# A decoder layer on one core: the mixers' output operands are read early and in pieces, and SyncE's issues keep the program's order inside the slots

## The chip, the core and the metric

The kernel runs on one core of a Trainium2 chip. Its engines are TensorE (PE in the profile, with its weight loads as PEld), VectorE (DVE), ScalarE (ACT), GpSimd (POOL) and SyncE (SP), which here issues the DMAs. The metric is the device time of one execution in microseconds.

## The reference, cut

One layer of a decoder, 1024 tokens of width 1024, everything in float32. Two groups of heads mix the tokens side by side, four mLSTM heads of width 128 and eight forgetting-attention heads of width 64. Their outputs are joined, multiplied by `w_out` and added to `x`. Cross-attention into 256 memory tokens and a squared-ReLU MLP follow.

```python
mh = mlstm_chunkwise(mq, mk, mv, ig, lf)          # 4 heads
ml_out = (mh.reshape(B, S, ML_W) * jax.nn.sigmoid(ml_o))
fx_out = forgetting_attention(fq, fk, fv, flf)    # 8 heads, causal, decayed
x = x + jnp.concatenate([ml_out, fx_out], axis=-1) @ w_out[l]
x = x + cross_attention(rmsnorm(x, ln_x[l]), rmsnorm(mem, ln_mem[l]), w_xq[l], w_xkv[l], w_xo[l])
u = jax.nn.relu(rmsnorm(x, ln2[l]) @ w_ff1[l])
x = x + (u * u) @ w_ff2[l]
return rmsnorm(x, ln_f)
```

## The kernel before

Activations lie with features on the 128 partitions and tokens along the row, in two halves of 512 tokens (`hf`). A float32 product is made of three matmuls of split operands (`mm3`, L192 to L194): each operand is cut into a high part, made by ScalarE (L138, or L971 in the slots), and a low part, the difference, made by VectorE or GpSimd (L139, L972).

The stage of interest is the forgetting stage, built of slots. Each call of `slot` does one value step of attention (transposes L793, the product with the values L813) and one score step some 13 slots ahead (L754, L755; maximum L761; exponential L767; scaling L778). Beside these it runs a share of other work from a generator (`filler`), so that TensorE has something to do: eight key units and four value units of cross-attention, and then 16 output units (`out_unit`), which multiply `w_out`'s first five row blocks with the mixers' output. Output units 0 to 7 belong to the first half of the tokens, 8 to 15 to the second. A unit takes its weights from `wr`, two buffers of raw weights: `cut_half` (L971, L972) splits one in two halves, and after the second half `raw_load` (L959) reads the next into the buffer just freed.

The mixers' outputs go through a DRAM tensor `mix[hf, part, :, k]`, where k is the block of 128 features: k 0 to 3 from the mLSTM heads, stored before the stage, and one further k for each two forgetting heads, stored in it (`fx_store`, L828 and L829, from buffers `r_y` and `r_f`). The output units read k 0 to 4 back. Before the change this happens when the first unit of each half runs (and for the second half at unit 4): `mix_load` (L875) reads four blocks into a buffer of the `act` pool, 1024 KB for each part, and `mix_tile` (L881) reads the fifth into a `z` buffer.

The queries and keys of the forgetting heads also come back from DRAM (`fqk`, `decay`), eight reads for a head, into two stacks of operands that heads use in turn. `score_parts` puts the reads of head hd+2 into a list `coming` when head hd has been scored, and each slot issues one of them (`fx_step`, L728). The list also carries the eight reads of `x`'s first half into `kept`, to which the output units of the first half add their sums. The units of the second half read their piece of `x` (L932) into small buffers `r_p`, `r_b`, `r_a` and store the sums in `x1d` (L942). After the slots, `mix_load` reads the remaining three blocks (768 KB a part), and `out_rest` finishes the product.

What sets the order: the code is traced, and a scheduler places each engine's instructions by its own reckoning. Inside the slots `in_order` ties each instruction of TensorE, ScalarE, VectorE and GpSimd to the one traced before it on the same engine. SyncE was not among them, so its issues stood where the scheduler put them. SyncE works off its queue in order: an issue that waits holds all behind it.

Of the kernel before, what the change touches and what calls it, by code (L numbers as in the profile page):

```python
# [9 lines left out]
F32 = mybir.dt.float32  # L10
F32R = mybir.dt.float32r
# [5 lines left out]
COMPUTE = (mybir.EngineType.PE, mybir.EngineType.Activation, mybir.EngineType.DVE, mybir.EngineType.Pool)  # L17
P = 128
T = 1024
TH = 512  # L20
D = 1024
KT = D // P
NM = 256
MLH = 4
FXH = 8
# [3 lines left out]
KX = 1  # L29
# [15 lines left out]
def hybrid_layer(ctx: ExitStack, tc: tile.TileContext, a: dict, out: bass.AP):  # L45
# [13 lines left out]
    def sb(tag, shape, bufs, dt=F32):  # L59
        return pool.tile(shape, dt, tag=tag, name=name(tag), bufs=bufs)  # L60

    def act(dt=F32R):
        return sb("act", [P, 8, TH], 7, dt)
# [8 lines left out]
    def w4(shape=(P, 1024), dt=F32):  # L72
        t = sb("w4", [P, 1024], 5, dt)[: shape[0]]
        return t.rearrange("p (a b) -> p a b", b=shape[2]) if len(shape) == 3 else t

    def z4():
        return sb("z4", [P, T + 3], 2)
# [24 lines left out]
    def mm():  # L102

        tag = banks[turn[0] % len(banks)]
        turn[0] += 1
        return ps_tile(tag)
# [4 lines left out]
    load = nc.sync.dma_start  # L111
# [33 lines left out]
    last_of = {}  # L145

    @contextmanager
    def in_order():

        traced = nc.cur_bb.bb.instructions  # L150
        last = traced[-1]
        yield
        start = next(k for k in reversed(range(len(traced))) if traced[k] is last) + 1
        for i in traced[start:]:
            if i.engine not in COMPUTE:
                continue
            if i.engine in last_of:
                tc.add_manual_dep(
                    i,
                    last_of[i.engine],  # L160
                    mybir.DependencyInfo(mybir.DependencyClass.NoSync, mybir.DependencyReason.DATA),
                    reason="in_order",
                )
            last_of[i.engine] = i.name


    def rotate(*tags):

        spare[tags] = spare.get(tags, -1) + 1
        return w2(tags[spare[tags] % len(tags)])  # L170
# [25 lines left out]
    def both(pair, f):  # L196
        return f(pair[0]), f(pair[1])
# [137 lines left out]
    for k in range(KT):  # L335
        if k % 2 == 0:
            c = slice(k % 4 * 256, k % 4 * 256 + 512)
# [44 lines left out]
    z, e, q, lf = (small[:, i:j].rearrange("p (t c) -> p t c", c=c) for i, j, c in ((0, 128, GC), (128, 224, GW), (224, 320, GW), (320, 416, GW)))  # L382
# [192 lines left out]
    mix = dram.tile([2, 2, P, KT, TH], F32, name="mix")  # L575
# [129 lines left out]
    for _ in range(2):  # L705
        t = act().rearrange("p a b -> p (a b)").rearrange("p (i c) -> p i c", i=4)
# [5 lines left out]
    coming = []  # L712

    def fx_load(hd):

        n, e = divmod(hd, 2)
        hs = stacks[hd % 2]
        rng = slice(e * FXD, e * FXD + FXD)
        lo_, up = slice(0, FXD), slice(FXD, P)
        for rows_, i, which, part in ((lo_, 0, 0, 0), (up, 0, 0, 1), (lo_, 1, 1, 0), (up, 1, 1, 0), (up, 2, 0, 0), (up, 3, 1, 1)):  # L720
            coming.append((hs[rows_, i], fqk[which, part, n, rng, :]))
        for at_, i, sign in ((0, 2, 0), (32, 3, 1)):
            coming.append((hs[at_ : at_ + 2, i], decay[sign, :, MLH + hd, :]))
# [105 lines left out]
        load(mix[hf, 1, :, MLH + hd // 2], lo.bitcast(F32))  # L829

    rooms = {}

    def score_parts():

        for hd in range(FXH):
            for hf in range(2):
                if hf:
                    t = act(F32).rearrange("p a b -> p (a b)").rearrange("p (i c) -> p i c", i=4)
                    rooms[hd, hf] = [t[:, d, : (5 + d) * P] for d in range(4)]
                else:  # L840
                    t = [w4((P, 2, TH)) for _ in range(2)]
                    rooms[hd, hf] = [t[d // 2][:, d % 2, : (1 + d) * P] for d in range(4)]
                for d in range(4):
                    x = Tile(hd, 4 * hf + d, rooms[hd, hf][d])
                    for e in range(len(x.parts)):
                        yield x, e
            if hd + 2 < FXH:
                fx_load(hd + 2)
            if 0 < hd < 5:
                coming.extend((kept[:, n], a["x"][:, n, :TH]) for n in (2 * hd - 2, 2 * hd - 1))  # L850

    def fv_load(hd):
        t = w4((P, 8, P), F32R)
# [18 lines left out]
    def mix_load(k0, k1, hf):  # L872
        t = act().rearrange("p (e k) c -> p e k c", e=2)
        for p_ in range(2):
            load(t[:, p_, : k1 - k0].bitcast(F32), mix[hf, p_, :, k0:k1])  # L875
        return [(t[:, 0, k], t[:, 1, k]) for k in range(k1 - k0)]

    def mix_tile(k, hf):
        t = z4()[:, :T].bitcast(F32R).rearrange("p (e c) -> p e c", e=2)
        for p_ in range(2):  # L880
            load(t[:, p_].bitcast(F32), mix[hf, p_, :, k])  # L881
        return t[:, 0], t[:, 1]

    late = []

# [34 lines left out]

        return [a["w_xv"][hd, i] for i in range(2)], run

    mixes = {}

    def out_unit(hf, n):
        def run(ws):
            if n == 0 and hf == 0 or n == 4 and hf == 0:
                mixes[n // 4] = mix_load(0, MLH, n // 4) + [mix_tile(k, n // 4) for k in range(MLH, MLH + KX)]
            x = kept[:, n]
            if hf:  # L930
                x = rotate("p", "b", "a", "p", "b")
                load(x, a["x"][:, n, TH:])  # L932
            w = both(ws[0], lambda t: t.rearrange("p (k c) -> p k c", k=MLH + KX))
            ps = mm()
            for k in range(MLH + KX):
                mm3(ps, both(w, lambda t: t[:, k]), mixes[hf][k], k == 0, k == MLH + KX - 1)
                yield 3.0, k == MLH + KX - 1, lambda: sink(x, ps)

        def sink(x, ps):
            v.tensor_tensor(out=x, in0=ps, in1=x, op=ALU.add)  # L940
            if hf:
                load(x1d[:, n], x)  # L942

        return [a["w_out_a"][n]], run
# [51 lines left out]
    stores, topped = [], []  # L996

    def slot(values, until):
        with in_order():
            todo_ = late[:]  # L1000
            late.clear()
            closing = bool(ended)
            sums = []
            while ended:
                sums.append(fx_close(*ended[0]))
                hd, hf, _ = ended.pop(0)
                if hd % 2:
                    stores.append((hd, hf, True))
            x = next(steps_, None) if values else None
            if x:  # L1010
                x.turn()
            mask()

            while adds and not closing and len(adds) >= (LAG if x else 1):
                y = adds.pop(0)
                y.add()
                if y.last:
                    ended.append((y.hd, y.hf, y.ov))
                    break
            tops = scored[:]  # L1020
            scored.clear()
            for t, e in tops:
                t.top(e)
            if x:
                x.cut()
                adds.append(x)
            for f in sums:
                f()
            exps = topped[:]
            topped[:] = tops  # L1030
            for t, e in exps:
                t.exp(e)
            while exped:
                exped.pop(0).scale()
            exped.extend(t for t, e in exps if e == len(t.parts) - 1)
            fx_step()
            part = next(parts, None)
            if part:
                part[0].score(part[1])
                scored.append(part)  # L1040
            late.extend(filter(None, [f() for f in todo_]))
            if stores and stores[0][2]:
                stores[0] = (*stores[0][:2], False)
            elif stores:
                fx_store(*stores.pop(0)[:2])
            while spent[0] < until:
                step = next(fill, None)
                if step is None:
                    break
                spent[0] += step[0]  # L1050
                if step[1]:
                    late.append(step[2])
                    break
            n, e = divmod(halves[0], 2)
            if until and n < len(sources) and (e or sum(u >= now[0] for u, _ in sources[:n]) < 3):
                cut_half()
        return x
# [9 lines left out]
    token_major(a["w_fv"], fv_sink, between={4: lambda: next(closing, None)})  # L1067
    hm = act().rearrange("p a b -> p (a b)").rearrange("p (e k c) -> p e k c", e=2, k=KT)
    kept = act(F32)
    load(hm.bitcast(F32), hmd)  # L1070
    banks[:] = ["mm", "m2"]
    raw_load()
# [2 lines left out]
    n = 0  # L1075
# [7 lines left out]
    for step in fill:  # L1083
        n, e = divmod(halves[0], 2)
# [246 lines left out]
    for n in range(KT):  # L1331
# [7 lines left out]
        k = n % 4  # L1339
# [150 lines left out]
    for at, (p_, i) in enumerate(jobs):  # L1490
# [19 lines left out]
        b, k = todo[p_][:2]  # L1510
# [53 lines left out]
    for at, (b, m) in enumerate(steps):  # L1564
# [14 lines left out]
        x = x2[m // 2][:, m % 2]  # L1579
# [16 lines left out]
    for i in range(2):  # L1596
        t = act()
# [132 lines left out]
```

## Time and profile before

| what | value |
|---|---|
| three runs, median (lowest, highest) | 1522.5 us (1521.36, 1523.13) |
| profiled execution | 1519.66 us |
| its span, first to last instruction | 1517.6 us |
| TensorE busy | 1501.4 us, 99% of the span |
| VectorE, ScalarE, GpSimd busy | 1103.2, 716.6, 438.5 us |
| DMA | 288.32 MB, 190 GB/s on average |
| granted TensorE clock | 0.998 |

A page of the profile gives such sums over the whole execution. The views used below are the lists of waits (who waited for whom, in total, how often, the longest), the timelines (start, duration, engine, line, output and inputs; in brackets the idle time of the engine before it and what ended it) and windows (busy times of the engines in a stretch). A row of SyncE in a timeline is the issue of a DMA, not its transfer. Busy TensorE is an upper figure, since matmuls overlap and their ends are modelled.

### The profile page before, as it was taken

How to read it: one execution, taken by the hardware profiler on the slowest of the kernel's cores; microseconds unless marked ns; L12 is line 12 of the kernel's file. 1: busy time of each engine (PE TensorE's matmuls, PEld its weight loads, DVE VectorE, ACT ScalarE, POOL GpSimd, SP SyncE). 2: the span in 40 equal slices, each digit the busy share in tenths (PEclk: the TensorE clock that was granted, in tenths of full speed). 3: DMA queues.
4: the chain of work that ended last, by engine and by line, in shares of the span. 5: the costliest groups of instructions: out<-in, count | busy, mean ns of one | idle time of the engine just before them, and what ended most of it. 6: DMA issues, size and time to landing. Idle time of an engine off the chain costs nothing.

```text
span 1517.6 us, 21814 instructions
## 1 busy us (share of the span) xinstructions
PE 1501.4 (99%) x7708; PEld 1259.1 (83%) x7708; DVE 1103.2 (73%) x1741; ACT 716.6 (47%) x1345; POOL 438.5 (29%) x497
## 2 busy tenths in 40 slices
PE   9999999999999999999999999999999999999997
PEld 8888888889898888888888887788888888888887
DVE  7676676665798875844457888788887788777765
ACT  7343343334678763543443456565556432222124
POOL 0003030413455541011110033343333544333312
PEclk9999999999999999999999999999999999999999
DMA  6332323436897928634333436776775966555623
GB/s 212 112 115 89 118 100 124 133 125 179 253 296 225 310 89 285 228 108 130 124 110 126 163 122 237 276 276 238 273 254 215 364 260 222 222 222 214 256 85 111
DMA packets 113489, 288.32 MB, mean 190 GB/s; under 512 B 12626, under 2 KB 27276, under 8 KB 107236
## 3 DMA queue, kind: packets, MB, share of 16 engines
q1 hardware_dynamic: 113092, 286.82, 55.4%
q8 instruction: 60, 0.98, 0.3%
q14 instruction: 49, 0.40, 0.1%
q10 hardware_dynamic: 288, 0.11, 0.0%
HBM read 194.36 MB, written 92.53 MB: 189 GB/s over the span
## 4 chain that ended last, share of the span: by engine, by line
PE 61%; DVE 2%; DMA 2%; issue 1%; ACT 1%; POOL 1%; SPq 0%; POOLq 0%; DVEq 0%; ACTq 0%
PE sc L192 5%; PE sc L194 5%; PE sc L193 5%; PE tp L192 5%; PE tp L194 5%; PE tp L193 5%; PE m L193 4%; PE m L192 4%; PE m L194 4%; PE mm L193 4%; PE mm L192 4%; PE mm L194 4%; PE ov L192 2%; PE ov L194 2%; PE ov L193 2%
## 5 line engine op out<-in xcount | busy, mean ns | idle before, releaser
L193 PE MATMUL tp<-act,wh 128*128 128x512 f32 (+1 forms) x456 | 178.7, 392 | 0.0
L192 PE MATMUL tp<-act,wl 128*128 128x512 f32 (+1 forms) x456 | 178.6, 392 | 0.0
L194 PE MATMUL tp<-act,wh 128*128 128x512 f32 (+1 forms) x456 | 178.5, 392 | 0.0
L138 ACT ACTIVATE wh<-wr 128x1024 fp32r<-128x1024 f32 (+3 forms) x96 | 92.7, 967 | 98.4 <-PE tp L194 36.5
L139 DVE TENSOR_TENSOR wl<-wr,wh 128x1024 fp32r<-128x1024 f32 (+3 forms) x96 | 114.3, 1192 | 15.3 <-ACT wh L138 15.2
L192 PE MATMUL mm<-act,wl 128*128 128x512 f32 (+1 forms) x320 | 122.8, 384 | 0.0
L193 PE MATMUL mm<-act,wh 128*128 128x512 f32 (+1 forms) x320 | 122.5, 383 | 0.0
L194 PE MATMUL mm<-act,wh 128*128 128x512 f32 (+1 forms) x320 | 122.2, 382 | 0.0
L192 PE MATMUL m<-act,wl 128*128 128x512 f32 (+1 forms) x312 | 119.6, 383 | 0.3 <-DVE wl L139 0.3
L193 PE MATMUL m<-act,wh 128*128 128x512 f32 (+1 forms) x312 | 119.0, 381 | 0.7 <-DMA act<-mix 0.7
L194 PE MATMUL m<-act,wh 128*128 128x512 f32 (+1 forms) x312 | 119.0, 381 | 0.0
L192 PE MATMUL sc<-act,wl 128*128 128x512 f32 (+1 forms) x268 | 103.9, 388 | 0.0
L193 PE MATMUL sc<-act,wh 128*128 128x512 f32 (+1 forms) x268 | 103.7, 387 | 0.0
L194 PE MATMUL sc<-act,wh 128*128 128x512 f32 (+1 forms) x268 | 103.7, 387 | 0.0
L194 PEld LDWEIGHTS tp<-act,wh 128*128 128x128 f32 x456 | 85.7, 188 | 19.5
L192 PEld LDWEIGHTS tp<-act,wl 128*128 128x128 f32 x456 | 85.7, 188 | 19.1 <-DVE w L1374 0.3
L193 PEld LDWEIGHTS tp<-act,wh 128*128 128x128 f32 x456 | 85.8, 188 | 18.8
L1464 POOL TENSOR_TENSOR z<-wr 128x256 f32<-128x256 f32 x56 | 54.1, 986 | 147.1 <-DMA wr<-w_ff2q 135.2
L138 ACT ACTIVATE w<-wr 128x768 fp32r<-128x768 f32 (+2 forms) x31 | 25.5, 824 | 132.1 <-PE tp L194 69.1
L138 ACT ACTIVATE wh<-z 128x1024 fp32r<-128x1024 f32 (+2 forms) x55 | 52.5, 956 | 65.7 <-POOL z L1464 30.5
L139 DVE TENSOR_TENSOR wl<-z,wh 128x1024 fp32r<-128x1024 f32 (+2 forms) x55 | 65.9, 1199 | 11.3 <-ACT wh L138 11.2
L194 PEld LDWEIGHTS mm<-act,wh 128*128 128x128 f32 x320 | 60.1, 188 | 12.5
(673 smaller groups left out, 4197.3 us busy)
## 6 DMA issues: line engine op xcount, KB each, us to landing
act<-right SPq DMA_DIRECT2D x35, 1024.0 KB
right<-r_d SPq DMA_DIRECT2D x70, 256.0 KB
right<-w SPq DMA_DIRECT2D x56, 256.0 KB
wr<-w_ff2q SPq DMA_DIRECT2D x28, 512.0 KB
act<-fqk SPq DMA_DIRECT2D x48, 256.0 KB
wr<-w_in SPq DMA_DIRECT2D x20, 512.0 KB
wr<-w_ff SPq DMA_DIRECT2D x20, 512.0 KB
fqk<-r_p SPq DMA_DIRECT2D x32, 256.0 KB
```

The source lines that it names most:

```text
L138: s.activation(hi, src, AF.Copy)
L139: return v.tensor_tensor(out=lo, in0=src, in1=hi.bitcast(F32), op=ALU.subtract)
L192: nc.tensor.matmul(ps, w[1], x[0], start=first, stop=False, skip_group_check=more)
L193: nc.tensor.matmul(ps, w[0], x[1], start=False, stop=False, skip_group_check=more)
L194: nc.tensor.matmul(ps, w[0], x[0], start=False, stop=last, skip_group_check=more)
L1464: g.tensor_tensor(out=o, in0=x, in1=y, op=op)
```

## The change

Three things. `in_order` takes the engines as an argument, and a slot passes SyncE too, as long as it has a value step or is one of the 13 slots before the first value step; the slots after the last value step don't. `mix_load` and `mix_tile` for the output units give way to `mix_ahead`, which claims the buffers of a half and returns ten reads of one block and one part each, 256 KB. The list `extra` says after which head's score step they join `coming`: the first half's ten after heads 2, 3 and 4, the second half's ten after head 6. The eight reads of `x`'s first half are spread anew, after heads 1, 4 and 5.

```diff
-    def in_order():
+    def in_order(engines=COMPUTE):
...
-            if i.engine not in COMPUTE:
+            if i.engine not in engines:
                 continue
...
-            if 0 < hd < 5:
-                coming.extend((kept[:, n], a["x"][:, n, :TH]) for n in (2 * hd - 2, 2 * hd - 1))
+            if hd == FXH - 2:
+                extra[hd].extend(mix_ahead(1))
+            coming.extend(extra[hd])
...
-    def mix_tile(k, hf):
-        t = z4()[:, :T].bitcast(F32R).rearrange("p (e c) -> p e c", e=2)
-        for p_ in range(2):
-            load(t[:, p_].bitcast(F32), mix[hf, p_, :, k])
-        return t[:, 0], t[:, 1]
+    mixes = {}
+
+    def mix_ahead(hf):
+        t = act().rearrange("p (e k) c -> p e k c", e=2)
+        z = [z4()[:, :T].bitcast(F32R).rearrange("p (e c) -> p e c", e=2) for _ in range(KX)]
+        mixes[hf] = [(t[:, 0, k], t[:, 1, k]) for k in range(MLH)] + [(y[:, 0], y[:, 1]) for y in z]
+        return [(mixes[hf][k][p_], mix[hf, p_, :, k]) for k in range(MLH + KX) for p_ in range(2)]
...
     def out_unit(hf, n):
         def run(ws):
-            if n == 0 and hf == 0 or n == 4 and hf == 0:
-                mixes[n // 4] = mix_load(0, MLH, n // 4) + [mix_tile(k, n // 4) for k in range(MLH, MLH + KX)]
...
     def slot(values, until):
-        with in_order():
+        with in_order(COMPUTE + (mybir.EngineType.SP,) * (values or not until)):
...
     kept = act(F32)
+    residual = [(kept[:, n], a["x"][:, n, :TH]) for n in range(KT)]
+    operands = mix_ahead(0)
+    for hd, more in ((1, residual[:4]), (2, operands[:4]), (3, operands[4:8]), (4, operands[8:] + residual[4:6]), (5, residual[6:])):
+        extra[hd].extend(more)
```

TensorE's and GpSimd's instructions stand in the same order as before; on VectorE and ScalarE a few neighbours change places at the end of the stage. What moves is SyncE's queue. In the middle of the stage it read before (`wr` is a unit's weights, `fvd` the values of a head, `kxd` and `vxd` stores of the key and value units):

```order
L854 DMA w4_798_4731<-fvd_512 128x1024
L828 DMA mix_509<-r_y_794_4715 128x512
L919 DMA vxd_96<-r_p_793_4711 256x1x256
L829 DMA mix_509<-r_f_690_4252 128x512
L881 DMA z4_1134_6201<-mix_509 128x512
L959 DMA wr_804_4761<-w_xv 128x1024
L881 DMA z4_1134_6201<-mix_509 128x512
L959 DMA wr_818_4823<-w_xk 128x1024
```

Now the same weights (`wr_806`) stand there like this:

```order
L923 DMA vxd_96<-r_p_795_4715 256x1x256
L828 DMA mix_509<-r_y_796_4719 128x512
L829 DMA mix_509<-r_f_692_4254 128x512
L856 DMA w4_800_4735<-fvd_512 128x1024
L728 DMA act_500_3176<-fqk_511 64x1024
L959 DMA wr_806_4765<-w_xv 128x1024
L728 DMA act_500_3176<-fqk_511 64x1024
L728 DMA act_500_3176<-decay_508 2x1024
L959 DMA wr_820_4827<-w_xk 128x1024
L728 DMA act_500_3176<-decay_508 2x1024
L728 DMA act_589_3833<-mix_509 128x512
```

The two reads of `mix` into `z` (L881), which fetch the block that the two stores above them (L828, L829) write, are gone from the weights' neighbourhood; a read of values and a read of the next head's queries stand ahead of the weights instead.

At the end of the stage, where the first output units of the second half add `x`, SyncE's queue before (`x1d` is the store of a unit's sum):

```order
L959 DMA wr_1229_6607<-w_out_a 128x640
L875 DMA act_1269_6846<-mix_509 128x1536 x2
L942 DMA x1d_3184<-r_p_1221_6574 128x512
L959 DMA wr_1244_6680<-w_out_a 128x640
L828 DMA mix_509<-r_y_1246_6688 128x512
L932 DMA r_p_1261_6780<-x 128x512
L829 DMA mix_509<-r_f_1200_6492 128x512
L942 DMA x1d_3184<-r_b_1240_6658 128x512
```

and now:

```order
L959 DMA wr_1229_6619<-w_out_a 128x640
L877 DMA act_1269_6858<-mix_509 128x1536 x2
L942 DMA x1d_3184<-r_p_1221_6586 128x512
L932 DMA r_b_1240_6670<-x 128x512
L959 DMA wr_1244_6692<-w_out_a 128x640
L932 DMA r_b_1257_6766<-x 128x512
L828 DMA mix_509<-r_y_1246_6700 128x512
L932 DMA r_p_1261_6792<-x 128x512
L829 DMA mix_509<-r_f_1200_6504 128x512
```

The reads of `x` into `r_b` for units 1 and 4 of the second half, which stood near the stage's beginning before, now stand here, the first behind the store of unit 0's sum.

More of the change, by code (lines that the diff above doesn't have):

```diff
@@ L831, in hybrid_layer @@
     rooms = {}
+    extra = [[] for _ in range(FXH)]
     def score_parts():
@@ L921, in value_unit @@
         return [a["w_xv"][hd, i] for i in range(2)], run
-    mixes = {}
     def out_unit(hf, n):
         def run(ws):
-            if n == 0 and hf == 0 or n == 4 and hf == 0:
-                mixes[n // 4] = mix_load(0, MLH, n // 4) + [mix_tile(k, n // 4) for k in range(MLH, MLH + KX)]
             x = kept[:, n]
```

## The prediction

> **What bounds the kernel now.** I read the page first, then the list of waits of TensorE and of its weight loads, then the timelines around each wait that the change can touch, and back from those to SyncE.
>
> From the page: the span and the busy times of the whole program.
>
> ```profile
> span 1517.6 us, 21814 instructions
> PE 1501.4 (99%) x7708; PEld 1259.1 (83%) x7708; DVE 1103.2 (73%) x1741; ACT 716.6 (47%) x1345; POOL 438.5 (29%) x497
> ```
>
> TensorE is the bound: 1517.6 - 1501.4 = 16.2 us of the span are not matmul. A change that leaves its instructions and their order alone, as this one does, can win only idle time of TensorE in the forgetting stage (391 to 578 us) and what follows it. The next view is the waits of the weight loads between 391 and 606 us (who, for whom: us in total, times, the longest). I take these because matmuls overlap and a short hold shows there more fully.
>
> ```profile
> PEld sc L754 <- ACT act L767: 3.5, 3, 2.2
> PEld tp L793 <- DVE r_e L139: 2.2, 3, 1.1
> PEld m L193 <- DMA act<-mix: 1.1, 1, 1.1
> PEld tp L793 <- DVE w L139: 0.6, 2, 0.5
> PEld sc L754 <- ACT w L767: 0.6, 1, 0.6
> ```
>
> Together 8.0 us: that is all that there is to win, half a percent. Two single waits are the largest, 2.2 and 1.1 us. TensorE's timeline shows both (start, duration; in brackets the idle time before and who ended it):
>
> ```profile
> 456.51 0.40 PE L813 MATMUL ov<-r_d,w 128*128 128x512 f32 x1
> 458.68 0.50 PE L754 MATMUL sc<-act 128*128 128x512 f32 x1 [1.77 <-ACT act L767]
> ...
> 507.56 0.40 PE L192 MATMUL m<-act,wl 128*128 128x512 f32 x1
> 508.63 0.50 PE L193 MATMUL m<-act,wh 128*128 128x512 f32 x1 [0.67 <-DMA act<-mix]
> ...
> 584.06 0.39 PE L194 MATMUL m<-z,wh 128*128 128x512 f32 x1
> 584.29 0.40 PE L192 MATMUL mm<-act,wl 128*128 128x512 f32 x1
> ```
>
> Each matmul is 512 columns wide. The last two rows show undisturbed ones of that width: they start 0.23 us apart. So the first hold cost 458.68 - 456.51 - 0.23 = 1.94 us and the second 508.63 - 507.56 - 0.23 = 0.84 us.
>
> **The cause of the first hold.** ScalarE's exponentials were late because it stood waiting for a weight tile; its timeline:
>
> ```profile
> 453.05 0.26 ACT L767 ACTIVATION_READ_ACCUMULATOR act<-sc,c_mx 128x1 f32 x1
> 457.06 0.63 ACT L971 ACTIVATE wh<-wr 128x512 fp32r<-128x512 f32 x1 [3.75 <-DMA wr<-w_xv]
> ```
>
> That tile's buffer was free when VectorE ended the subtraction that last read it; the read was issued only at 453.07, after a read of the mixers' output. VectorE's row, then SyncE's timeline, then the row of SyncE's own waits:
>
> ```profile
> 448.49 0.86 DVE L972 TENSOR_TENSOR wl<-wr,wh 128x512 fp32r<-128x512 f32 x1 [0.37 <-ACT wh L971]
> 449.88 0.32 SPq L829 DMA_DIRECT2D mix<-r_f  x1
> 452.65 0.32 SPq L881 DMA_DIRECT2D z<-mix  x1
> 453.07 0.37 SPq L959 DMA_DIRECT2D wr<-w_xv  x1
> ...
> SPq L881 <- DMA mix<-r_y: 2.4, 1, 2.4
> ```
>
> The buffer was free at 448.49 + 0.86 = 449.35. SyncE came to the read of mix (L881) at 450.2, waited 2.4 us until the store of the same bytes had landed, and the weights behind it left 3.72 us late. ScalarE waited 3.75 us, TensorE 1.94 us: there were about 1.8 us of slack between them.
>
> **The change, part by part.** (a) Order within the slots. In the new order the read of mix into z is gone from this place; ahead of the weights now stand the two stores, a 512 KB read of values and one 256 KB read of queries. None of these needs a store of this moment, and all belong to work earlier in the slot than the subtraction that frees the weights' buffer. So the weights leave at about 449.4 instead of 453.07. Even if the values ahead of them cost 1 us in the queue, the read lands 2.6 us earlier, more than the hold. I take the whole 1.94 us; the bounds are 0 (the queue eats it, a rival below) and the 2.2 us of the weight load's row.
>
> (b) The mixers' operands for the first half are read in ten pieces of 256 KB, eight of them before that half's first unit. They were read in one go when the first output unit began:
>
> ```profile
> 498.93 1.34 SPq L875 DMA_DIRECT2D act<-mix  x2
> ```
>
> TensorE wanted them at 507.79 (507.56 + 0.23) and waited until 508.63. The two last pieces (z) go out in the slots in which the unit starts and are wanted by its fifth step, three slots later. The stage's transposes, first and last, give the length of its slots (min/median/max of one in ns, then the first and the last start):
>
> ```profile
> L793 PE MATMUL tp<-ident,act x208: 270/272/329, 395.9 to 576.4; 128*128 128x128 f32 x104
> L793 PE MATMUL tp<-ident,w x80: 270/273/329, 391.3 to 563.5; 128*128 128x128 f32 x80
> ```
>
> From 391.3 to 576.4 run 95 slots, 1.95 us each. Three are some 5.8 us, and 256 KB have taken 5.4 at the worst (below). So the 0.84 us goes whole. Bounds: 0 and the 1.1 us of its weight load's row.
>
> (c) What is late next. Four reads of x for the second half were free to go far ahead before; now the one for unit n=1 (r_b, L932) stands behind the store of unit 0's sum (x1d from r_p), which stands behind two reads of 768 KB (mix, L875). SyncE's timeline, its wait, and VectorE's add of that unit:
>
> ```profile
> 574.79 1.78 SPq L875 DMA_DIRECT2D act<-mix  x2
> 577.92 0.32 SPq L942 DMA_DIRECT2D x1d<-r_p  x1
> 583.31 0.33 SPq L932 DMA_DIRECT2D r_p<-x  x1
> ...
> SPq L932 <- DMA x1d<-r_p: 2.1, 1, 2.1
> ...
> 581.53 0.68 DVE L940 TENSOR_TENSOR r_b<-mm,r_b 128x512 f32<-128x512 f32 x1
> ```
>
> The queue at that time, first as a window (length, busy times by engine, clock, DMA share, GB/s), then by the slowest read in it, a weight tile's issue and the instruction that waited for it:
>
> ```profile
> 578.00:606.00 28.00, 28.00 (x123) 22.56 (x122) 12.26 (x17) 6.56 (x13) 3.86 (x5) 1.00 0.95 330
> ...
> 588.52 0.38 SPq L959 DMA_DIRECT2D wr<-w_out_a  x1
> ...
> 595.72 0.83 ACT L971 ACTIVATE wh<-wr 128x320 fp32r<-128x320 f32 x2 [5.66 <-DMA wr<-w_out_a]
> ```
>
> The store issued at 577.92 landed at 583.3: 5.4 us, behind 1.5 MB. A 256 KB read issued right behind it lands 0.8 us later (at the window's 330 GB/s), at 584.1. The add (0.68 us) then ends at 584.8, not 582.2, and TensorE, which starts unit 3 in that same bank at 584.29 (the row above), waits 0.5 us, with the semaphore 0.6. So +0.6 us; bounds 0 (lands by 583.6) and 2.0 (lands as late after its issue at 578.4 as that slowest read, 595.72 - 588.52 = 7.2 us: 585.6, add ends 586.3).
>
> (d) The 36 reads of queries and keys, before in bursts, now go one per slot; so do the eight reads of x for the first half. All land ahead of their use by the working in the first rival: 0. The extra issues (12 more reads, the same bytes) at about 0.4 us each are SyncE's time, which has nothing else queued: 0. The weight subtraction moved ahead of r_b's add on VectorE, and one split of the next stage moved behind a squaring; no wait of TensorE lies there: 0.
>
> Sum: -1.94 - 0.84 + 0.6 = -2.18 us. Against the profiled execution (1519.66 us, span 1517.6) that gives 1517.5; that run lay 2.84 us under the median of the three, 1522.5, so I put the difference on the median: **1520.3 us**.
>
> [...] Two more windows:
>
> ```profile
> 422.00:432.00 10.00, 9.93 (x76) 9.19 (x75) 9.27 (x21) 9.26 (x25) 5.13 (x6) 1.00 0.99 338
> 440.00:513.00 73.00, 69.91 (x509) 64.76 (x508) 63.34 (x157) 57.12 (x161) 39.00 (x60) 1.00 0.86 260
> ```
>
> From 422 to 432 us eight reads of 256 KB and a few of 512 KB moved 338 GB/s, as much as the 768 KB reads after 578 us (330): small pieces cost the queue nothing visible. [...]
>
> **The rivals.** First, slower: the stack rows of queries, keys and decay come too late. They were loaded in a burst; now the last of eight comes four slots before the head's first score, and SyncE reaches it only after a store of the same slot.
>
> ```profile
> 430.01 0.56 SPq L900 DMA_DIRECT2D kxd<-r_a  x1
> ...
> 436.45 0.28 PE L754 MATMUL sc<-act 128*128 128x256 f32 x1
> ```
>
> For head 3 the last row would leave at 430.6 (behind that store) and is wanted at 436.45: 5.85 us. It decides where landing takes longer. The 5.4 us above fit; the 7.2 us don't: 1.35 us late, for heads 3 to 7 five times, 6.8 us, so -2.2 + 6.8 = +4.6: 1527 us. For it: SyncE now stands still for every store. Against: bursts, which made landings slow, are gone. 17%.
>
> Second, no change: the weights land as late as before, since 512 KB of values and 256 KB of queries were put ahead of them; 1.94 us stay and only -0.84 + 0.6 = -0.24 remains: 1522.3 us. For it: the queue is 0.86 busy there. Against: 3.7 us of head start. 20%.
>
> Third, more: without bursts the other weights land earlier too and half of the remaining 8.0 - 2.2 - 1.1 = 4.7 us of waits goes: -2.18 - 2.35 = -4.5: 1518.0 us. Against: those waits end with VectorE, busy 63.34 of 73 us there. 18%.
>
> **How the numbers follow.** My forecast has 45%, 1519 to 1521.5. A difference under 0.2%, 3 us, is about what these timings can't tell from no change; its edges are 1519.5 and 1525.5. Faster: a third of my case, 15, and nearly all of the third rival, 17: 32%. Slower: the first rival but for a mild form, 15, and a little of the unforeseen: 16%. The rest, 52%, is within. The range reaches to the third rival with 1 us to spare and most of the way to the first: 1517.0 to 1526.0.
>
> **What would show it.** Right: no wait of score matmuls for L767 of over 1 us near 456 us; no wait for mix near 508; the weights' read within 0.5 us of the end of the subtraction that frees it; and a new wait of at most 1 us before unit 3's matmuls near 582 us, ended by L940. Wrong: waits of L754 for the stack reads at a head's first score (first rival), ScalarE still waiting over 3 us for w_xv (second), or a wait in a place that I named at nothing.

## The result: 1518.7 us, and the profile after

The changed kernel took 1518.68 us (median of 14 executions, 1516.9 to 1522.8), the kernel before 1522.1 us (14, 1519.59 to 1524.99) on the same chip: a ratio of 0.9982, with a 95% interval of 0.9974 to 0.999. On another chip the same kernel gave 0.9989 (0.9979 to 0.9998). By these ratios the change gains 2.7 and 1.7 us, at the edge of what these timings can tell from nothing. The median lies in the range that was forecast, 1.6 us under the forecast itself.

The profiled execution of the changed kernel tells another story. It took 1521.24 us, 1.6 us more than the profiled execution of before. From its page:

```profile
span 1519.5 us, 21816 instructions
...
PE 1502.5 (99%) x7708; PEld 1260.7 (83%) x7708; DVE 1103.0 (73%) x1741; ACT 716.8 (47%) x1345; POOL 441.5 (29%) x497
```

The waits of its weight loads between 391 and 606 us, the same view as in the prediction:

```profile
PEld sc L754 <- ACT act L767: 3.8, 2, 2.8
PEld tp L793 <- DVE r_e L139: 2.2, 3, 1.1
PEld mm L192 <- issue: 0.7, 1, 0.7
PEld tp L793 <- DVE w L139: 0.6, 2, 0.5
PEld sc L754 <- ACT w L767: 0.6, 1, 0.6
```

The wait for mix is gone, the wait for the bank mm has grown (0.2 us before, a row that the prediction's list leaves out), and the largest, which step (a) took away, is longer than before (2.8 against 2.2 us). SyncE's timeline shows why, and ScalarE's:

```profile
446.08 0.55 SPq L923 DMA_DIRECT2D vxd<-r_p  x1
446.74 0.55 SPq L828 DMA_DIRECT2D mix<-r_y  x1
447.38 1.02 SPq L829 DMA_DIRECT2D mix<-r_f  x1
448.49 0.40 SPq L856 DMA_DIRECT2D w<-fvd  x1
448.95 0.45 SPq L728 DMA_DIRECT2D act<-fqk  x1
449.50 0.53 SPq L959 DMA_DIRECT2D wr<-w_xv  x1
```

```profile
457.41 0.63 ACT L971 ACTIVATE wh<-wr 128x512 fp32r<-128x512 f32 x1 [4.31 <-DMA wr<-w_xv]
```

The weights' read left at 449.50, where I had put it (449.4), 3.57 us earlier than before. It was used at 457.41, later than before (457.06). It took 7.9 us, where before it took 4.0. Five transfers, 1.5 MB with the stores, were issued in the 3.4 us ahead of it. The queue's windows (length, busy times by engine, clock, DMA share, GB/s), first of the changed kernel, then of before:

```profile
448.00:452.00 4.00, 4.00 (x30) 3.74 (x30) 3.65 (x8) 4.00 (x12) 2.03 (x3) 1.00 0.96 281
452.00:456.00 4.00, 4.00 (x34) 3.82 (x32) 3.84 (x9) 1.10 (x3) 0.98 (x2) 1.00 0.99 257
```

```profile
448.00:452.00 4.00, 4.00 (x30) 3.75 (x30) 3.57 (x10) 4.00 (x12) 2.03 (x4) 1.00 1.05 382
452.00:456.00 4.00, 4.00 (x32) 3.77 (x31) 3.84 (x9) 1.31 (x4) 0.98 (x2) 1.00 0.72 232
```

With the read itself that is 2.1 MB, and at the 281 and 257 GB/s of the two windows they would take about 7.8 us, but that sum is not the account, since only 0.1 of the stores' 0.8 MB had still to move when the read was issued. The trace shows what was still ahead: each of these transfers lands in sixteen parts, and each part has its own record. The middle one of the sixteen stands at 450.27 us for the last store (`r_f`), at 452.50 for the values, at 454.03 for the queries and at 455.58 for the weights; the weights' last part landed at 457.39. So of the 7.9 us, 0.8 went to the stores, 2.2 to the values, 1.5 to the queries, 1.6 to the weights themselves and 1.8 to those of their parts that came late. Before, the last part of the values had landed at 452.00, ahead of the weights' issue; the weights' middle part stood at 456.72 and the last one at 457.04.

Why the full queue moved fewer bytes than before (257 GB/s at a share of 0.99 against 382 at 1.05) is not shown; it was not the stores, since from 452 to 456 us the queue moved reads alone. The transfers landed in the order in which they were issued (the last parts of the last store, the values, the queries and the weights at 450.77, 454.05, 455.10 and 457.39 us): the earlier issue bought a place behind the values and the queries.

TensorE's timeline then shows what came on top:

```profile
456.29 0.39 PE L813 MATMUL ov<-r_d,w 128*128 128x512 f32 x1
459.03 0.50 PE L754 MATMUL sc<-act 128*128 128x512 f32 x1 [2.36 <-ACT act L767]
...
461.79 0.63 PE L754 MATMUL sc<-act 128*128 128x512 f32 x1
462.21 0.63 PE L755 MATMUL sc<-act 128*128 128x512 f32 x1
```

After an idle time of 2.36 us, matmuls of 512 columns start 0.42 us apart, not 0.23. The windows by clock, of the changed kernel and of before:

```profile
456.00:460.00 4.00, 1.64 (x10) 1.12 (x9) 1.38 (x3) 2.59 (x8) 1.91 (x3) 1.00 0.67 201
460.00:465.00 5.00, 5.00 (x27) 4.60 (x26) 3.95 (x10) 3.31 (x10) 2.60 (x5) 0.66 0.74 229
```

```profile
460.00:465.00 5.00, 5.00 (x39) 4.52 (x38) 4.86 (x16) 4.52 (x14) 2.91 (x6) 1.00 0.84 242
```

A mean clock of 0.66 over 5 us is 3.4 us at half clock ((1 - 0.66) x 5 / 0.5), and the trace's clock record has 0.50 from 460.04 to 463.45 us. In the profiled execution of before the idle time was 1.77 us and the clock stayed at 1.00.

So two profiles cannot settle where the gain came from. The other two waits answer to the prediction. The operands of mix (b), no idle time at the first unit's start:

```profile
509.30 0.40 PE L192 MATMUL m<-act,wl 128*128 128x512 f32 x1
509.53 0.39 PE L193 MATMUL m<-act,wh 128*128 128x512 f32 x1
```

And the second half's first units (c), TensorE, then VectorE:

```profile
584.73 0.40 PE L194 MATMUL m<-z,wh 128*128 128x512 f32 x1
585.40 0.47 PE L192 MATMUL mm<-act,wl 128*128 128x512 f32 x1 [0.28 <-DVE r_b L940]
```

```profile
584.57 0.69 DVE L940 TENSOR_TENSOR r_b<-mm,r_b 128x512 f32<-128x512 f32 x1 [1.07 <-DMA r_b<-x]
```

The matmul of unit 3 started 0.67 us after the one before it instead of 0.23: 0.44 us lost, where 0.5 was forecast.

### The profile page after: what moved, and what is told of

Read it like the earlier page. It is cut to its first block, busy times and chain, and to the rows that moved or that the text cites. A ratio compares the mean times of both kernels' runs of the same rounds, so it can differ in the third digit from the quotient of the medians.

```text
span 1519.5 us, 21816 instructions
## 1 busy us (share of the span) xinstructions
PE 1502.5 (99%) x7708; PEld 1260.7 (83%) x7708; DVE 1103.0 (73%) x1741; ACT 716.8 (47%) x1345; POOL 441.5 (29%) x497
## 4 chain that ended last, share of the span: by engine, by line
PE 61%; DVE 3%; DMA 2%; issue 1%; ACT 1%; POOL 1%; SPq 0%; POOLq 0%; DVEq 0%; ACTq 0%
PE sc L192 5%; PE sc L194 5%; PE sc L193 5%; PE tp L192 5%; PE tp L194 5%; PE tp L193 5%; PE m L192 4%; PE m L194 4%; PE m L193 4%; PE mm L192 4%; PE mm L193 4%; PE mm L194 4%; PE ov L192 2%; PE ov L194 2%; PE ov L193 2%; PE ov L813 1%
```

## The experiments

Three theories stood after the result. *Issue* is step (a) as written: the earlier issue takes the hold away, and the profiled execution is an exception. *Queue* is the prediction's second rival: the weights land as late as before in every execution. *Clock* says that the hold lies near a length from which the clock halves, and that the kernels differ in how often that happens. "Slot 33" is the slot whose value tile starts near 456 us; it is the one in which ScalarE waits for w_xv. Every execution also has its mean granted clock on record.

**Both kernels again.** No edit.

> The kernel before, unchanged, for a second profile. Three theories are told apart by this call. Issue: what is gained is the hold of TensorE at the weights of slot 33 (1.94 us near 457 us), because the read of w_xv leaves earlier; the one profile of the changed kernel, in which it landed late all the same, is an exception. Queue: the read lands late in every execution of the changed kernel, since 512 KB of values and 256 KB of queries went ahead of it; the gain is the wait for mix (0.84 us) less the tail (0.5 us) and nothing else is systematic. Clock: the hold near 457 us is near a length from which the granted clock halves for about 3.4 us afterwards (1.5 us lost); before trips it in most executions, the changed kernel in few, and the two profiles so far show each kernel's exception. Expected here: ratio to before 0.999 to 1.001 by all three. Issue and queue: a hold of 1.5 to 2.2 us, as in the first profile, and no half clock there. Clock: a stretch of half clock between 455 and 470 us where the profiled execution takes over 1521 us, none where it takes under 1520.

> The changed kernel, unchanged, for a second profile. Ratio to before 0.9974 to 0.999 by all three. Issue: the read of w_xv lands by 455 us and TensorE is held under 0.7 us before the scores near 457 us. Queue: it lands at 456.5 us or later, and TensorE is held 1.5 us or more. Clock: no half clock between 455 and 470 us where the execution takes under 1519.5 us; where there is one, over 1520.5 us.

Ratios 1.0001 (0.9992 to 1.0011) and 0.9989 (0.9979 to 0.9998). TensorE's row at the hold and the window behind it, both of the kernel before, then the row of the changed kernel:

```profile
460.12 0.67 PE L754 MATMUL sc<-act 128*128 128x512 f32 x1 [2.49 <-ACT act L767]
```

```profile
460.00:465.00 5.00, 4.88 (x22) 4.42 (x23) 4.16 (x11) 3.77 (x12) 1.96 (x4) 0.66 0.51 164
```

```profile
460.54 0.50 PE L754 MATMUL sc<-act 128*128 128x512 f32 x1 [2.53 <-ACT act L767]
```

Issue falls: the hold of the changed kernel is 2.5 us in the second trace too, and the read was again used late (458.92 us, issued at 451.30). But the kernel before has executions with the half clock as well.

**Each part alone.** Order alone: the kernel before with

```diff
-        with in_order():
+        with in_order(COMPUTE + (mybir.EngineType.SP,) * (values or not until)):
```

> One part alone: the kernel before, with SyncE's issues kept in program order within the slots; the mixers' operands are still read in one go at a half's first unit, and the reads of x for the first half stand where they stood. The wait for mix near 508 us stays (0.8 us or more, since the two z reads come later too) and the tail's wait near 582 us comes (0.5 us). Issue: -1.94 + 0.5 = -1.4 us, ratio 0.999. Queue: +0.5 us, ratio 1.0003. Clock: by how often the hold trips the gate, -1.5 + 0.5 to +0.5.

Measured 1530.48 us, ratio 1.0061 (1.0045 to 1.0078): 8 us slower, which no theory expected. TensorE's timeline at slot 33 and near the first output unit, the window behind that, and SyncE's timeline:

```profile
457.96 0.49 PE L754 MATMUL sc<-act 128*128 128x512 f32 x1 [0.76 <-ACT act L767]
...
512.66 0.77 PE L192 MATMUL m<-act,wl 128*128 128x512 f32 x1 [5.53 <-DMA act<-mix]
...
515.03 0.79 PE L193 MATMUL m<-act,wh 128*128 128x512 f32 x1 [1.61 <-DMA act<-mix]
```

```profile
514.00:519.00 5.00, 3.96 (x11) 3.14 (x12) 0.85 (x2) 1.79 (x6) 0.35 (x1) 0.54 0.34 131
```

```profile
504.23 0.36 SPq L959 DMA_DIRECT2D wr<-w_out_a  x1
504.64 0.90 SPq L728 DMA_DIRECT2D act<-x  x2
505.58 0.90 SPq L875 DMA_DIRECT2D act<-mix  x2
```

The two reads of mix, 1024 KB each, left at 505.58 us; before, they had been taken out of order and left at 498.93. TensorE stood 7.1 us for them, and the clock was 0.54 from 514 to 519 us. The idle time at slot 33, though, was only 0.76 us in this trace: with the same five transfers ahead, the weights' read took 5.8 us. The order alone may help there, and it loses far more here; the pieces are what makes the order bearable.

Pieces alone: the changed kernel with the diff above turned round.

> The other part alone: the changed kernel, with SyncE's issues left to the scheduler. The read of mix into z no longer stands ahead of w_xv here, but the 512 KB of values do, and five reads of queries and keys; the four reads of x for the second half are free to go ahead again, so the tail's wait near 582 us goes. Issue: -1.94 - 0.84 = -2.8 us, ratio 0.9982, the weights leave within 0.5 us of the end of the subtraction that frees them. Queue: -0.84 us, ratio 0.9994, the weights land at 456.5 us or later. Clock: -0.84 or -2.3 us.

Measured 1521.88 us, ratio 0.9998 (0.9988 to 1.0007). The wait for mix is gone, TensorE's idle time at slot 33 is 1.55 us in the trace; three reads of mix stood just ahead of the weights there, and the weights' read took 5.7 us. The ratio is what queue expected (0.9994), and not issue (0.9982).

**The wrong tile.** The next experiment was to read the held tile early, into a spare buffer:

```diff
             src = sources[n][1]
+            if n == AHEAD:
+                raws_.append(ahead)
+                return
...
+    AHEAD, ahead = 6, z4()[:, :1024]
+    coming.append((ahead, sources[AHEAD][1]))
```

> The changed kernel, with one 512 KB weight tile (the half of w_xv that ScalarE waits for near slot 33) read some 40 us earlier into a spare buffer of 4 KB, so that no read of weights is asked for in a hurry there. The bytes are the same. Issue (my step a as written: the changed kernel had already taken that hold away): same time as the changed kernel, ratio to before 0.9985. Queue (the weights landed late in the changed kernel since the bytes ahead of them share the queue): the hold of 2.9 to 3.2 us near 457 us falls under 0.5 us, so about 2.5 us less than the changed kernel, ratio 0.997. Clock: TensorE is never idle for over 2 us there, so no execution shows the half clock between 455 and 475 us; the slowest timed execution lies under 1521 us, where the changed kernel's lay at 1522.9.

> The same early read in the kernel before, nothing else changed. The wait for mix near 508 us stays (0.5 to 1.1 us). Issue: the hold is 1.94 us and goes, -1.9 us, ratio 0.9987. Queue: the same. Clock: the half clock goes too, in about six executions of ten in which it had tripped (mean granted clock 0.996 or less): 1.94 + 0.6 x 1.5 + a longer hold in those (3.4 instead of 1.9) = -3.7 us, ratio 0.9976, and the spread of the times shrinks from 5.7 us to about 3.

> Both edits on the changed kernel: the weight tile read ahead, and the program order kept only until slot 86. Issue: 0.998. Queue and clock: 0.9967, 5 us under the kernel before, the fastest of all, with no hold over 1 us between 440 and 606 us except at the transposes of slot 51.

The number was wrong: tile 6 is cut a head earlier; the tile that ScalarE waits for is number 10. Both kernels behaved as without the edit: 0.9992 (0.9982 to 1.0002) for the changed one, 1.0004 (0.9995 to 1.0013) for before, 0.9987 (0.9978 to 0.9996) with the free tail. As tests of the theories they are void, but they give three more traces of the hold: idle times of 1.13 and 1.67 us in the two variants of the changed kernel, at full clock, and in before:

```profile
459.78 0.50 PE L754 MATMUL sc<-act 128*128 128x512 f32 x1 [2.10 <-ACT act L767]
```

```profile
460.00:465.00 5.00, 5.00 (x26) 4.51 (x25) 3.82 (x10) 3.43 (x10) 1.99 (x4) 0.66 0.57 174
```

**The tail.** The changed kernel, program order on SyncE until slot 86 only:

```diff
-(mybir.EngineType.SP,) * (values or not until)
+(mybir.EngineType.SP,) * bool(values and until < 84 * 3.6 or not until)
```

> The changed kernel, with SyncE's program order kept only until slot 86 of 96, so that the four reads of x for the second half go far ahead again. The wait of TensorE before unit 3 near 585 us (0.5 to 0.7 us, ended by the add of L940) goes. All theories: 0.5 us less than the changed kernel, ratio to before 0.998; a difference of that size may not show in the times, so the verdict rests on the trace.

Ratio 0.999 (0.9981 to 0.9999): the time shows nothing, as was said. In the trace the add of r_b starts at 580.86 and no longer waits for its read, and unit 3 is not held behind it. The cause in (c) is right. It is also the trace with the longest idle time that did not halve the clock:

```profile
458.95 0.50 PE L754 MATMUL sc<-act 128*128 128x512 f32 x1 [1.93 <-ACT act L767]
```

```profile
460.00:465.00 5.00, 5.00 (x39) 4.52 (x38) 4.86 (x15) 4.52 (x14) 2.69 (x5) 1.00 0.75 245
```

**The held tile.** The same edit with `AHEAD = 10`, in the changed kernel, in before, with the free tail, and in the kernel with the pieces alone.

> The early read once more, now of the tile that ScalarE waits for near slot 33 (the eleventh weight tile of the stage; the two runs before moved the seventh, which was not the one). Changed kernel otherwise. Queue and clock: ScalarE does not wait for w_xv near 457 us, the stall of slot 33 (1.6 to 3.2 us in the four traces of the changed kernel and its variants) falls under 0.7 us, no half clock between 455 and 475 us, 2.5 + 0.5 = 3 us less than the changed kernel, ratio to before 0.9967. Rival: another weight tile takes its place (the next one, of w_xk, leaves only when this one's slot is reached, some 2 us before its use) and TensorE is held 1 to 2 us a few slots later: 0.998.

> The same in the kernel before. Its stall at slot 33 (2.2 to 3.8 us in three traces) goes and with it the half clock that followed in two of three: 3 + 0.6 x 1.5 = 3.7 us less, ratio 0.9976; the wait for mix near 508 us stays at 0.5 to 1.1 us. Rival: 0.999, since the next tile is late instead. If this kernel is as fast as the changed one, then the hold at slot 33 is worth at least as much as everything that the change does.

> Changed kernel, the held tile read ahead, and SyncE's program order kept only until slot 86 of 96. 0.5 us less than with the tile alone: 0.9964, and the fastest of all. Rival (next tile late): 0.9977.

> The pieces without the program order, with the held tile read ahead. If the program order is worth something only through the read of the weights at slot 33, it is worth nothing here, and this kernel runs like the one with the free tail: 0.9964. If it orders other reads usefully, this kernel is slower than that, 0.998.

| kernel, tile 10 read ahead | median us (executions) | ratio to before | interval |
|---|---|---|---|
| changed | 1517.58 (7) | 0.9971 | 0.996 to 0.9982 |
| before | 1517.33 (7) | 0.9971 | 0.9961 to 0.9982 |
| changed, free tail | 1516.84 (7) | 0.9966 | 0.9956 to 0.9977 |
| pieces alone | 1516.78 (6) | 0.9967 | 0.9955 to 0.9979 |

In the kernel before, ScalarE takes the tile from the spare buffer without a wait, TensorE runs through slot 33, and of its weight loads' waits the largest that are left are others:

```profile
452.41 0.69 ACT L974 ACTIVATE wh<-z 128x512 fp32r<-128x512 f32 x1
```

```profile
455.79 0.39 PE L813 MATMUL ov<-r_d,w 128*128 128x512 f32 x1
456.02 0.40 PE L754 MATMUL sc<-act 128*128 128x512 f32 x1
```

```profile
PEld tp L793 <- DVE r_e L139: 2.4, 4, 1.1
PEld m L193 <- DMA act<-mix: 1.1, 1, 1.1
```

No rival wait of a next tile came. Slots 33 and 34 together, by TensorE's timeline, from the start of slot 33's first transpose to slot 35's, are 4.34 to 4.35 us long in these four traces. They are 5.5 to 6.6 us in the six traces that had the hold at full clock, and 8.2 to 8.6 us in the four in which the clock halved. So the wait on one 512 KB tile costs this kernel 1.1 to 2.3 us, or about 4 us where the clock halves behind it.

Two things follow. One early read in the kernel before wins at least as much as the whole change (ratio 0.9971 against 0.9982 and 0.9989; that it wins more is likely, but the intervals overlap). And with that read in both, the changed kernel and the kernel before take the same time, to the 1.6 us or so that each interval leaves on either side: apart from slot 33 the change is worth nothing that shows. The mix wait that it removes and the tail wait that it adds partly cancel.

## Why the prediction came out right, and where it was wrong

**(a), -1.94 us: the issue right, the landing wrong.** The weights left at 449.50 us as worked out, and the hold stayed (2.36 and 2.53 us idle in the two traces of the changed kernel). The step that failed is "Even if the values ahead of them cost 1 us in the queue, the read lands 2.6 us earlier". It put 1 us on the values, and nothing on the queries, on the stores still under way and on the read's own late parts. By the landings these took 2.2, 1.5, 0.8 and 1.8 us (the late parts 0.3 us before), and the read took 3.9 us longer than before, more than its 3.57 us of head start. In the five traces of the changed kernel and its variants without tile 10 ahead the read took 6.5 to 7.9 us, in three of the kernel before (one with the wrong tile moved) 4.0 to 4.1 us, and TensorE's idle time at slot 33 was 1.92 against 2.12 us on average. The mechanism of the second rival, given 20%, is what the traces show.

**That rival's time, 1522.3 us, did not come either.** It had left the clock out, as I had. The six traces with an idle time under 2 us at slot 33 kept the full clock there; the four with 2.10 us or more all ran 3.4 us at half clock, and slots 33 and 34 took some 2 us longer. How often that happens can be read only roughly from the mean clocks, since a stretch at half clock at the program's end varies too (8.1 us in the first trace of the changed kernel, 5.1 us in that of before), and one of the four traces with the half clock at slot 33 has 0.997. Of the kernel before (with the variant that moved the wrong tile), 54 of 104 executions have 0.996 or less; of the changed kernel and its three variants without tile 10 ahead, 18 of 61; with tile 10 ahead, 1 of 27. By these counts the clock halves less often in the changed kernel (30% against 52%), though it did behind the hold in both of its own profiled executions. At 2 us each that makes some 0.45 us; with 0.2 us of shorter idle time and 0.4 us of (b) and (c) it makes about 1 us of the 1.7 to 2.7 us measured. This is argued from counts and from few traces; what the rest is, no run shows, and the intervals of the two ratios alone span 0.3 to 4 us. Why the read's landing differs by 1 to 2 us between executions is open.

**(b), -0.84 us: right.** The wait is gone in every trace with the pieces. It stays with order alone and in the kernel before, with tile 10 ahead too (1.1 us in the weight loads' row above). In the second trace of before that row has only 0.5 us, so the mean is somewhat under my 0.84.

**(c), +0.6 us: right in place, cause and size, though not in every execution.** 0.44 us in the first trace, 0.7 in the kernel with tile 10 ahead (0.50 idle), none in the second trace of the changed kernel. The semaphore, 0.1 us in the prediction, took 0.14 in the first trace (the add ended at 585.26, the matmul started at 585.40).

**(d), 0: right** for what it named. No score waits for the stack rows; the first rival did not come.

**The pieces in the queue: nothing that shows,** as the prediction said. With them the queue was about as busy between 440 and 513 us as without, 0.88 against 0.86 at 251 against 260 GB/s.

**The sum** of -2.18 us against the -1.7 to -2.7 us measured is therefore partly luck: (b) and (c) together give about -0.4 us of it in the first trace. Of the rest, as much as is found came through slot 33, in good part by the clock, of which the prediction does not speak.

## What to carry to other kernels

Before you count an earlier issue as an earlier landing, list what will still be in the queue ahead of it, stores too, give each transfer the time that it takes in that window (here 2.2 us for 512 KB of values, 1.5 us for 256 KB of queries), and allow for late parts of the read itself (1.8 us here). When one transfer holds the matmul engine, move that transfer by tens of microseconds into a spare buffer, if there is one, rather than reorder the queue around it. And ordering a queue can make large late reads later, as it did here (505.58 against 498.93 us), so split and hoist these first, then order.

## What the runs showed of the hardware

Inside this stage's stream of matmuls the clock halved for 3.4 us after TensorE had been idle for 2.10, 2.36, 2.49 and 2.53 us, and did not after 0.76, 1.13, 1.55, 1.67, 1.77 and 1.93 us. With the four holds behind which it halved, slots 33 and 34 were 8.2 to 8.6 us long, about 4 us more than the 4.3 us without a hold, and the half clock is a thing of single executions: the kernel before shows it in two of its three traces without tile 10 ahead.

Whether the length of the wait alone decides, these ten traces do not show. In the clock record of the first trace of the changed kernel the half clock at slot 33 lasts 3.413 us, and there and in the record of the first trace of before each stretch of full clock lasts a whole multiple of that (453.97 and 1047.89 us, 133 and 307 times, in the changed kernel; 1505.28 us, 441 times, in before).

Each of the transfers of 256 and 512 KB followed above landed in sixteen parts, and ScalarE took the weights only after the last of these (457.41 us behind 457.39 in the changed kernel, 457.06 behind 457.04 in before). The last part of the weights landed 1.81 us behind the middle one in the first trace of the changed kernel, 0.32 us in the first of before.
